# A hybrid decoder layer: the mixers' SBUF in two pools, the SwiGLU's first operands in three groups, and large GpSimd work on VectorE

## The chip, the core and the metric

One core of a Trainium2 chip runs the whole layer. The metric is the device time in microseconds (us) of one execution. The engines are PE (TensorE), DVE (VectorE), ACT (ScalarE), POOL (GpSimd) and SP, which here only issues DMAs; each works through its own queue in order. PEld is the weight load of PE.

## What is computed

```python
h   = x * (1 + scale1) + shift1                 # x: 2048 tokens x 1024
p   = h @ W_in                                  # 26 blocks of 128 columns
mix = concat(conv3_gated(p[:12 blocks]), rwkv7(p[12:])) @ W_out
x   = LayerNorm(alpha * x + (1 + gate1) * mix)
h   = x * (1 + scale2) + shift2
gate, up = split(h @ W_ffn_in)                  # 1024 -> 2 * 2816
x   = LayerNorm(alpha * x + (1 + gate2) * ((silu(gate) * up) @ W_ffn_out))
```

shift, scale and gate come from a small matrix product with c. Everything is float32.

## The kernel before

**Products in three terms.** Each float32 operand is split into a rounded high half and the rest (`split`, L230 to L233: a cast on ACT, then a subtraction), and each product is three matmuls of 128x512. The rest of a weight is `l` for W_in, `lo` for W_out and `wl` for the SwiGLU.

**Mixers.** The tokens come in four quarters of 512. A quarter has projections (`dense`, L256, whose weights `half_weight`, L249, loads and splits) and four units of two RWKV heads each (`unit`, L436), a long chain of small matmuls with DVE and ACT work between them. Within a unit, `kP`, `BK`, `rk` and `R` are products of two 128x512 SBUF tiles. `out_proj` (L301) multiplies a finished quarter by W_out; its matmuls are `do`. Quarters 0 and 1 are projected during the mixers, 2 right behind them, 3 some blocks into the SwiGLU. Normalised and modulated tokens go to DRAM as `h2d`.

**SwiGLU.** Both large products use seven block products instead of eight (`PRODS`, L967). The first product works in two halves of 1024 tokens. `moving` (L1048) loads a half's blocks `b` from `h2d` (four per k, with k from 0 to 3), forms sums and differences of two blocks (`bh`, `us`; L988 on DVE), and splits them into `uh` (ACT) and `ul` (DVE or POOL by turns): 28 operands, two tiles each. Then 22 column blocks run, each seven products of 12 matmuls named `f`; a DVE or ACT instruction takes each product out of PSUM (`c`, L1007).

```python
PRODS = (                                   # product, weight blocks, token blocks
    (3, ("11",), ("12", "-22")),   (5, ("11", "12"), ("22",)),
    (1, ("11", "22"), ("11", "22")), (4, ("22",), ("21", "-11")),
    (7, ("12", "-22"), ("21", "22")), (2, ("21", "22"), ("11",)),
    (6, ("21", "-11"), ("11", "12")))
```

During the second half, `scale_weights` (L1164) loads W_ffn_out in 44 pieces of 128x512 (`wf`, two buffers), multiplies each by the gate's row and stores it to `wfs`.

**What sets the order.** PE's order is written out by `Interleave`, which mixes the projections and the units by a table of assumed delays. For the other engines a scheduler orders the instructions when the program is built. SBUF is given out in pools: `rw` holds all of the mixers' tiles, and after it `fa`, at the same addresses, the SwiGLU's. A tile of `fa` waits for the tiles of `rw` that lay there, and the scheduler gives out the pool after the last of `rw`.

Of the kernel before, what the change touches and what calls it, by code (L numbers as in the profile page):

```python
# [11 lines left out]
F32 = mybir.dt.float32  # L12
F32R = mybir.dt.float32r
AF = mybir.ActivationFunctionType
ALU = mybir.AluOpType
# [4 lines left out]
P = 128  # L20
# [8 lines left out]
QT = S // NQ  # L29
C = 64  # L30
# [41 lines left out]
class Interleave:  # L72
# [31 lines left out]
    def __call__(self, stream, last=True):  # L104

        more = True
        while more or any(last or not t[3] for t in self.tasks):
            if self.side():
                continue
            cost = next(stream, 0) if more else None  # L110
            if cost == 0:
                more = False
            elif cost is not None:
                self.now += cost
            elif self.tasks and not self.side():
                self.now = min(t for t in [t[0] for t in self.tasks] + self.banks if t > self.now)


@with_exitstack
def kernel(  # L120
# [21 lines left out]
    act, dve, pool, pe = nc.scalar, nc.vector, nc.gpsimd, nc.tensor  # L142
# [87 lines left out]
    def split(hi, lo, raw, lo_eng=None):  # L230

        act.copy(out=hi, in_=raw)  # L232
        (lo_eng or pool).tensor_sub(lo, raw, hi)  # L233
# [8 lines left out]
    lnp = ctx.enter_context(tc.tile_pool(name="lnp", bufs=1))  # L242
# [7 lines left out]
    def half_weight(src, name):  # L250

        raw = f512("raw", "r" + name, 3)
        load(out=raw, in_=src)
        wh = f512("wh", "h" + name, 4, F32R)
        wl = f512("wl", "l" + name, 4, F32R)
        split(wh, wl, raw)  # L256
        return wh, wl

    def dense(mov, *tiles):
# [109 lines left out]


    with ExitStack() as ph1:
        rw = ph1.enter_context(tc.tile_pool(name="rw", bufs=1))
        dsc = ph1.enter_context(tc.tile_pool(name="dsc", bufs=1, space=DRAM))


# [16 lines left out]
        uph = rw.tile([P, 512], F32R, name="uph")  # L392
        upl = rw.tile([P, 512], F32R, name="upl")
        gu = rw.tile([P, 512], F32, name="gu")
        blkr = rw.tile([P, P], F32R, name="blkr")

        for tag, bufs in (("yc", 1), ("yo", 1), ("sg", 2)):
            rw.tile([P, QT], F32, tag=tag, name="at" + tag, bufs=bufs)

        carry = rw.tile([P, 2, 14], F32, name="carry")  # L400
        dve.memset(carry, 0.0)
        zcar = rw.tile([P, 4, 2], F32, name="zcar")
# [32 lines left out]
        def c3(ap):  # L435
            return ap.rearrange("p (c t) -> p c t", t=C)  # L436

        def unit(n, q, hp, r, kx, vx, lo):
            u = f"{q}_{hp}"
            th, tl, sg = lo  # L440
# [21 lines left out]
            tz = t2k("tz", "tz" + u)  # L462
# [4 lines left out]
            Pi = t2k("Pi", "Pi" + u)  # L467
            act.activation(Pi, cum, AF.Exp, scale=KAPPA)

            ta = t2k("ta", "ta" + u)  # L470
            act.activation(ta, psa, AF.Tanh, bias=a0h[:, hp:hp + 1], scale=0.5)
            x1, x2 = t2k("nb", "x1" + u), t2k("x2", "x2" + u)
            for x, (m, o) in ((x1, halves[0:2]), (x2, halves[2:4])):
                dve.tensor_scalar(x, ta, m[:, hp:hp + 1], o[:, hp:hp + 1], ALU.mult, ALU.add)
            mk = ta
            act.activation(mk, ta, AF.Identity, scale=kah[:, hp:hp + 1], bias=omka[:, hp:hp + 1])

            sq = t2k("sq", "sq" + u)
# [11 lines left out]
            kP = Pi  # L490
            dve.tensor_tensor(out=kP, in0=Pi, in1=kx, op=ALU.mult)
            BK = rw.tile([P, NC_Q, 2 * C], F32, tag="BK", name="BK" + u, bufs=1)
            dve.tensor_tensor(out=BK[:, :, 0:C], in0=c3(kP), in1=c3(x1), op=ALU.mult)
            pool.tensor_tensor(out=BK[:, :, C:2 * C], in0=c3(kP), in1=c3(x2), op=ALU.mult)

            rk = t2k("sq", "rk" + u)
            pool.tensor_tensor(out=rk, in0=kx, in1=mk, op=ALU.mult)
            dve.scalar_tensor_tensor(out=rk, in0=rk, scalar=vecs[:, V_RK + hp:V_RK + hp + 1], in1=r,
                                     op0=ALU.mult, op1=ALU.mult)
            rkh, rkl = (t2k(tag, f"rk{x}{u}", 1, F32R) for x, tag in (("h", "nb"), ("l", "Pi")))  # L500
# [9 lines left out]
            dve.scalar_tensor_tensor(out=Ak, in0=c3(kx), scalar=nkk[:, hp:hp + 1], in1=Pc[:, :, 0:C],  # L510
                                     op0=ALU.mult, op1=ALU.mult)
            R = rw.tile([P, NC_Q, C], F32, tag="R", name="R" + u, bufs=2)
            pool.tensor_tensor(out=R, in0=c3(r), in1=Pc[:, :, 1:C + 1], op=ALU.mult)


            VU = rw.tile([P, NC_Q, 2, C], F32, tag="VU", name="VU" + u, bufs=2)
# [208 lines left out]
            yo = t2k("yo", "yo" + u)  # L725
# [30 lines left out]
        class Inputs:  # L756


            def __init__(self, q):
                self.q, self.got = q, []  # L760
# [271 lines left out]
        return psum.tile([P, 512], F32, tag=tag, name=name, bufs=bufs)  # L1032

    with ExitStack() as ph2:
        fa = ph2.enter_context(tc.tile_pool(name="fa", bufs=1, reuse_waits="tile"))

        for tag, bufs in (("h26", 8), ("h22", 8), ("h27", 8), ("h24", 8), ("h21", 8), ("h25", 8), ("rawx", 4),
                          ("h23", 8), ("us", 1)):
            fa.tile([P, 512], F32, tag=tag, name="at" + tag, bufs=bufs)
        U = {}  # L1040

        def cycle(*makers):
# [3 lines left out]
        def moving(half):  # L1046

            def operand(i, k, terms, raws, n):  # L1050
                hi, lo = [fa.tile([P, 512], F32R, tag=f"h2{i}", name=f"u{x}{half}_{i}_{k}", bufs=8) for x in "hl"]
                U[half, i, k] = combine(raws, terms, hi, lo, sums, (dve, pool)[n % 2])

            def fetch(t, name, k):
                kk, n = 4 * (int(name[0]) - 1) + k, int(name[1]) - 1
                t0 = half * HT + n * 512
                load(out=t, in_=h2d[kk, :, t0:t0 + 512])
                return t

            def own():  # L1060
                return fa.tile([P, 512], F32, tag="us", name=f"us{half}", bufs=1)

            names = ("12", "22", "11", "21")
            hb = lnp.tile([P, 2, 512], F32, tag="hb", name=f"bh{half}", bufs=1)
            if half == 0:
                sums = cycle(lambda: hb[:, 0, :], lambda: hb[:, 1, :], own)
                for k in range(4):
                    raws = {}
                    for b in names:
                        t = (lnp.tile([P, 512], F32, tag="xr", name=f"b{k}_{b}", bufs=2) if b == "21" else  # L1070
                             fa.tile([P, 512], F32, tag="rawx", name=f"b{k}_{b}", bufs=4))
                        raws[b] = fetch(t, b, k)
                    for n, (i, _, terms) in enumerate(PRODS):
                        operand(i, k, terms, raws, n + k)
                return
            xz = lnp.tile([P, 4, D], F32, tag="xz", name="bz", bufs=1)
            slots = [xz[:, i // 2, i % 2 * 512:(i % 2 + 1) * 512] for i in range(8)] + [hb[:, 0, :], hb[:, 1, :]]
            slots += [lnp.tile([P, 512], F32, tag="xr", name=f"bx{i}", bufs=2) for i in range(2)]
            slots += [temp(f"bt{i}") for i in range(4)]
            sums = cycle(lambda: temp("us"), own)  # L1080
            raws = {k: {} for k in range(4)}
            for b in names:
                for k in range(4):
                    raws[k][b] = fetch(slots.pop(0), b, k)
            yield
            for i, _, terms in PRODS:
                for k in range(4):
                    operand(i, k, terms, raws[k], k)
                yield
# [73 lines left out]
        rw3 = []  # L1163

        def scale_weights():

            for ff in range(FT):
                for m in range(2):
                    ms = slice(m * 512, (m + 1) * 512)
                    w = lnp.tile([P, 512], F32, tag="xr", name=f"wf{ff}_{m}", bufs=2)  # L1170
                    load(out=w, in_=wfo[ff, :, ms])
                    pool.tensor_tensor(out=w, in0=w, in1=rw3[0][:, ms], op=ALU.mult)  # L1172
                    load(out=wfs[ff, :, ms], in_=w)
                    yield

# [239 lines left out]
```

## Time and profile before

| | |
|---|---|
| time, median of 3 runs | 2881.92 us (2880.78 to 2887.45) |
| the profiled execution | 2881.27 us; span of its instructions 2879.5 us |
| PE busy | 2660.8 us, 92% of the span |
| DVE, POOL, ACT busy | 1898.7, 1148.7, 1098.7 us |
| mean granted TensorE clock | 0.955 of 2.4 GHz |
| DMA | 369.86 MB, 128 GB/s over the span |

A time in the text is counted from the first instruction of the span. The mixers run to 1401 us, the SwiGLU's first product from there to about 2390 us, its second to the end. A row that groups instructions gives their line, engine, operation, output<-inputs, shape and count; behind the first bar the busy time in us and the mean ns of one, behind the second the engine's idle time before them and what ended it.

### The profile page before, as it was taken

Reading aid. Unit: us, or ns where it says so; the run is one execution under the profiler, and the core shown is the slowest. Engines: PE = TensorE matmul, PEld = TensorE weight load, DVE = VectorE, ACT = ScalarE, POOL = GpSimd, SP = SyncE. Lnnn points to the kernel's source line nnn. Section 1 sums busy time; section 2 is a strip of 40 time slices with the busy share of each in tenths; the row PEclk is TensorE's granted clock in tenths of the full one; section 3 lists DMA queues with packets and bytes.
Section 4 is the critical chain, followed back from the end, with each engine's and each line's share of the span. In section 5 each row is a group of like instructions: output and inputs, shape, how many; then the busy total and the mean of one; then the engine's idle time right before and its main releaser. Section 6 shows DMA issues by size and latency. Waiting matters only on the chain.

```text
span 2879.5 us, 50206 instructions
## 1 busy us (share of the span) xinstructions
PE 2660.8 (92%) x19232; PEld 2082.8 (72%) x19232; DVE 1898.7 (66%) x3133; ACT 1098.7 (38%) x1995; POOL 1148.7 (40%) x935
## 2 busy tenths in 40 slices
PE   7788999999999899998599999997999999998998
PEld 5566677776777677766477788875767887887786
DVE  7354655556445655554573777788988778659697
ACT  4554433334432433434353533333223333332352
POOL 4665333323333333332453544457886442000011
PEclk8888999989999999999799999998999999999999
DMA  6443322233322222224253533233664336655673
GB/s 236 139 129 116 91 62 70 73 104 119 120 69 69 84 66 69 77 72 156 92 179 128 169 105 106 99 99 121 219 213 138 107 102 222 207 179 186 202 237 106
DMA packets 248344, 369.86 MB, mean 128 GB/s; under 512 B 58660, under 2 KB 81188, under 8 KB 248104
## 3 DMA queue, kind: packets, MB, share of 16 engines
q1 hardware_dynamic: 248104, 366.65, 39.5%
q8 instruction: 151, 2.47, 0.3%
q14 instruction: 89, 0.73, 0.1%
HBM read 278.99 MB, written 87.56 MB: 127 GB/s over the span
## 4 chain that ended last, share of the span: by engine, by line
PE 40%; DVE 5%; DMA 4%; POOL 2%; issue 1%; ACT 0%; SPq 0%; POOLq 0%; DVEq 0%; ACTq 0%
PE f L238 8%; PE f L237 8%; PE f L236 8%; PE o L237 4%; PE o L238 4%; PE o L236 4%; PE do L270 3%; DMA wf<-in_wfo_dram 2%; DMA wfs<-wf 2%; POOL wf L1172 1%; DVE c L1007 1%; DVE ws L988 1%; DMA b<-h2d 0%; DVE ul L233 0%; POOL wl L233 0%
## 5 line engine op out<-in xcount | busy, mean ns | idle before, releaser
L236 PE MATMUL f<-uh,wh 128*128 128x512 f32 x1232 | 495.8, 402 | 32.2 <-ACT uh L232 27.7
L238 PE MATMUL f<-uh,wl 128*128 128x512 f32 x1232 | 495.1, 402 | 19.9 <-POOL wl L233 19.7
L237 PE MATMUL f<-ul,wh 128*128 128x512 f32 x1232 | 494.0, 401 | 12.0 <-DVE ul L233 7.2
L233 POOL TENSOR_TENSOR l<-r,h 128x512 fp32r<-128x512 f32 x201 | 265.2, 1321 | 444.8 <-ACT h L232 359.5
L233 POOL TENSOR_TENSOR wl<-ws,wh 128x512 fp32r<-128x512 f32 x220 | 316.3, 1439 | 296.7 <-ACT wh L232 259.5
L236 PEld LDWEIGHTS f<-uh,wh 128*128 128x128 f32 x1232 | 234.8, 191 | 92.8 <-ACT uh L232 31.8
L238 PEld LDWEIGHTS f<-uh,wl 128*128 128x128 f32 x1232 | 234.8, 191 | 85.6 <-POOL wl L233 30.5
L237 PEld LDWEIGHTS f<-ul,wh 128*128 128x128 f32 x1232 | 234.8, 191 | 72.2 <-DVE ul L233 9.4
L232 ACT CAST wh<-ws 128x512 fp32r<-128x512 f32 x220 | 136.7, 621 | 364.7 <-DVE ws L988 259.0
L1007 DVE TENSOR_TENSOR c<-f,c 128x512 f32<-128x512 f32 x264 | 181.2, 687 | 127.6 <-PE f L238 69.7
L988 DVE TENSOR_TENSOR ws<-w,w 128x512 f32<-128x512 f32 x275 | 242.8, 907 | 18.0 <-DMA w<-wfs 7.4
L237 PE MATMUL o<-ol,fh 128*128 128x512 f32 x616 | 243.3, 395 | 8.9 <-DVE ol L233 8.9
L236 PE MATMUL o<-oh,fh 128*128 128x512 f32 x616 | 242.1, 393 | 4.2 <-DVE c L1007 4.1
L238 PE MATMUL o<-oh,fl 128*128 128x512 f32 x616 | 243.7, 396 | 0.0
L232 ACT CAST h<-r 128x512 fp32r<-128x512 f32 x201 | 123.5, 616 | 215.6 <-PE d L270 157.5
L232 ACT CAST fh<-fr 128x512 fp32r<-128x512 f32 x154 | 95.7, 621 | 237.4 <-PE o L237 160.5
L291 POOL TENSOR_SCALAR rsb<-mvb 128x1 f32<-128x1 f32 x16 | 5.7, 356 | 430.2 <-DVE mvb L289 419.6
L233 DVE TENSOR_TENSOR fl<-fr,fh 128x512 fp32r<-128x512 f32 x154 | 106.2, 693 | 94.1 <-ACT fh L232 85.8
L233 POOL TENSOR_TENSOR lo<-ro,ho 128x512 fp32r<-128x512 f32 x64 | 83.6, 1312 | 198.3 <-ACT ho L232 148.4
L233 POOL TENSOR_TENSOR wl<-w,wh 128x512 fp32r<-128x512 f32 x88 | 127.4, 1448 | 49.4 <-ACT wh L232 49.4
L237 PEld LDWEIGHTS o<-ol,fh 128*128 128x128 f32 x616 | 116.7, 189 | 37.1 <-DVE ol L233 10.6
L236 PEld LDWEIGHTS o<-oh,fh 128*128 128x128 f32 x616 | 116.7, 189 | 31.3 <-DVE c L1007 5.7
(498 smaller groups left out, 5800.1 us busy)
## 6 DMA issues: line engine op xcount, KB each, us to landing
r<-in_win_dram SPq DMA_DIRECT2D x201, 256.0 KB
w<-in_wfi_dram SPq DMA_DIRECT2D x176, 256.0 KB
fr<-fd SPq DMA_DIRECT2D x154, 256.0 KB
w<-wfs SPq DMA_DIRECT2D x132, 256.0 KB
fd<-fs SPq DMA_DIRECT2D x110, 256.0 KB
wm<-in_wmod_dram SPq DMA_DIRECT2D x72, 256.0 KB
ro<-in_wout_dram SPq DMA_DIRECT2D x64, 256.0 KB
fd<-th SPq DMA_DIRECT2D x44, 256.0 KB
```

Of the source, the lines that this page charges most:

```text
L232: act.copy(out=hi, in_=raw)
L233: (lo_eng or pool).tensor_sub(lo, raw, hi)
L236: pe.matmul(ps, lh, rh, start=start, stop=False)
L237: pe.matmul(ps, lh, rl, start=False, stop=False)
L238: pe.matmul(ps, ll, rh, start=False, stop=stop)
L270: pe.matmul(ps, l[:, ks], r, start=kk == 0 and i == 0, stop=kk == KT - 1 and i == 2)
L291: pool.tensor_scalar(rs[:, 0:1], mv[:, 1:2], LN_EPS, None, ALU.add)
L988: (eng or dve).tensor_tensor(out=out, in0=blocks[a], in1=blocks[b.lstrip("-")], op=ALU.subtract if b[0] == "-" else ALU.add)
L1007: dve.tensor_tensor(out=c[b, t], in0=in0, in1=in1, op=op)
L1172: pool.tensor_tensor(out=w, in0=w, in1=rw3[0][:, ms], op=ALU.mult)
```

## The change

There are five edits.

1. The mixers' tiles lie in two pools, `rw` (left) for 20 tags that a unit uses early and `rwb` (right) for the others. `fa` follows at `rw`'s addresses with the loaded blocks `rawx`, one sum tile `us` and the operands of products 3 and 5 (`h23`, `h25`); `fab` follows at `rwb`'s with the other five products' operands. Empty tiles that had fixed the order of addresses are dropped.
2. `moving(0)` makes its operands in three groups, products 3 and 5, then 1 and 4, then 7, 2 and 6, each for all four k, and loads the blocks that a group needs: 8, 12 and 16 loads of 256 KB in place of 16 in all.
3. The low halves of the W_in and W_out weights are made on DVE.
4. In a unit, the second half of `BK`, the first product of `rk` and `R` are made on DVE.
5. The 44 products of `scale_weights` are made on DVE.

```diff
+class Pools:
+    def __init__(self, first, second, early):
+        self.pools, self.early = (second, first), early
+    def tile(self, shape, dtype, name, tag=None, bufs=1):
+        return self.pools[(tag or name) in self.early].tile(shape, dtype, tag=tag or name, name=name, bufs=bufs)
+EARLY1 = ("uph", "upl", "blkr", "Ak", "BK", "x2", "tz", "Pi", "ta", "nb", "sq", "cg", "r", "A", "th", "tl", "k", "v", "z", "AK")
+EARLY2 = ("rawx", "h23", "h25", "us")
...
-        split(wh, wl, raw)
+        split(wh, wl, raw, dve)
...
-        rw = ph1.enter_context(tc.tile_pool(name="rw", bufs=1))
+        rw = Pools(ph1.enter_context(tc.tile_pool(name="rw", bufs=1)),
+                   ph1.enter_context(tc.tile_pool(name="rwb", bufs=1, side="right")), EARLY1)
...
-            pool.tensor_tensor(out=BK[:, :, C:2 * C], in0=c3(kP), in1=c3(x2), op=ALU.mult)
+            dve.tensor_tensor(out=BK[:, :, C:2 * C], in0=c3(kP), in1=c3(x2), op=ALU.mult)
-            pool.tensor_tensor(out=rk, in0=kx, in1=mk, op=ALU.mult)
+            dve.tensor_tensor(out=rk, in0=kx, in1=mk, op=ALU.mult)
...
-            pool.tensor_tensor(out=R, in0=c3(r), in1=Pc[:, :, 1:C + 1], op=ALU.mult)
+            dve.tensor_tensor(out=R, in0=c3(r), in1=Pc[:, :, 1:C + 1], op=ALU.mult)
...
-        fa = ph2.enter_context(tc.tile_pool(name="fa", bufs=1, reuse_waits="tile"))
+        fa = Pools(ph2.enter_context(tc.tile_pool(name="fa", bufs=1, reuse_waits="tile")),
+                   ph2.enter_context(tc.tile_pool(name="fab", bufs=1, reuse_waits="tile", side="right")), EARLY2)
...
-                for k in range(4):
-                    raws = {}
-                    for b in names:
...
-                    for n, (i, _, terms) in enumerate(PRODS):
-                        operand(i, k, terms, raws, n + k)
+                for prods in (PRODS[:2], PRODS[2:4], PRODS[4:]):
+                    for k in range(4):
+                        raws = {}
+                        for b in names:
+                            if any(b in (x.lstrip("-") for x in terms) for _, _, terms in prods):
...
+                        for n, (i, _, terms) in enumerate(prods):
+                            operand(i, k, terms, raws, n + k)
...
-                    pool.tensor_tensor(out=w, in0=w, in1=rw3[0][:, ms], op=ALU.mult)
+                    dve.tensor_tensor(out=w, in0=w, in1=rw3[0][:, ms], op=ALU.mult)
```

PE's order stays as it was but for four small places. On the other queues instructions move; three places follow. In the rows, lines are those of the program shown (the change's are 10 to 14 higher), and a name's last number tells buffers apart.

SP at the end of the mixers, before. `yT<-yg_3` is the store of the last unit's result, `ro` are W_out's weights, `b` the SwiGLU's blocks and `w` its weights:

```order
L1100 DMA w_0_12_15127<-in_wfi_dram 128x512
L1100 DMA w_11_11_15289<-in_wfi_dram 128x512
L734 DMA yT<-yg_3_14536 128x512
L1057 DMA b_12_14955<-h2d 128x512
L1057 DMA b_22_14957<-h2d 128x512
```

And of the change, the stretch from the first blocks on:

```order
L267 DMA ro_5_1_14845<-in_wout_dram 128x512
L1065 DMA b_22_14952<-h2d 128x512
L1065 DMA b_12_14963<-h2d 128x512
...
L267 DMA ro_7_0_14873<-in_wout_dram 128x512
L1065 DMA b_11_15005<-h2d 128x512
...
L745 DMA yT<-yg_3_14536 128x512
L1065 DMA b_11_15055<-h2d 128x512
```

Two blocks (`b_21`) were ahead of that store before; now 18 are, and 18 follow it. The loads of `ro` stand among them.

DVE in the last projection of the mixers, of the change. `lo_4_1` is the low half of W_out that PE's `do` matmuls need next, `S_3` a step of the last unit's state, `mtt` a transposed output of `do`:

```order
L339 SCALAR_TENSOR_TENSOR xz_14673<-xz_14673,mtt_1_14703 128x4x128
L999 TENSOR_TENSOR bh_14949<-b_12_14950,b_22_14952 128x512
L247 TENSOR_TENSOR ul_3_0_14955<-bh_14949,uh_3_0_14954 128x512
L999 TENSOR_TENSOR bh_14949<-b_12_14963,b_22_14965 128x512
L247 TENSOR_TENSOR lo_4_1_14803<-ro_4_1_14800,ho_4_1_14802 128x512
L709 TENSOR_SCALAR S_3_14416<-s_3_14418,Pc_3_13378 128x64
```

Before, this stretch of DVE had only the `S_3` and `xz` rows; `lo_4_1` stood on POOL, and the sums of `b` stood behind the last unit's end.

DVE while W_ffn_out is scaled, of the change. `ws` are sums of weights, `c` takes a product from PSUM:

```order
L999 TENSOR_TENSOR ws_2_7_20409<-w_2_12_20298,w_2_22_20300 128x512
L1182 TENSOR_TENSOR wf_1_21403<-wf_1_21403,rws 128x512
L1018 TENSOR_TENSOR c_2_20426<-f_2_5_20413,c_2_20405 128x512
L999 TENSOR_TENSOR ws_2_2_20434<-w_2_21_20302,w_2_22_20300 128x512
L1182 TENSOR_TENSOR wf_0_21448<-wf_0_21448,rws 128x512
L1018 TENSOR_TENSOR c_2_20405<-f_2_1_20438,c_2_20405 128x512
```

Before, POOL had the `wf` rows, one or two between two `wl`. Now 141 other rows of DVE stand between the first `wf` and the last, 57 of them `c` rows, of which a column block has eight.

## Rows read from the trace of the kernel before

**Rows 1.** The page, part 1: busy us, share of the span, instructions.
```profile
PE 2660.8 (92%) x19232; PEld 2082.8 (72%) x19232; DVE 1898.7 (66%) x3133; ACT 1098.7 (38%) x1995; POOL 1148.7 (40%) x935
```
**Rows 2.** Windows: us, busy per engine (PE, PEld, DVE, ACT, POOL), PEclk, DMA share, GB/s.
```profile
72.00:360.00 288.00, 244.92 (x2384) 187.29 (x2386) 149.15 (x272) 136.91 (x248) 159.32 (x132) 0.88 0.40 119
360.00:1300.00 940.00, 893.85 (x10011) 683.64 (x10007) 516.61 (x1092) 356.75 (x683) 326.56 (x294) 0.97 0.27 81
...
1401.00:1465.00 64.00, 28.81 (x96) 19.86 (x96) 48.72 (x63) 29.76 (x49) 35.74 (x29) 0.65 0.39 130
1465.00:1930.00 465.00, 458.20 (x2006) 369.81 (x2005) 331.20 (x436) 178.94 (x327) 222.01 (x170) 1.00 0.38 126
...
1993.00:2180.00 187.00, 171.73 (x707) 131.98 (x706) 164.75 (x161) 52.69 (x91) 164.38 (x102) 0.99 0.64 215
```
**Rows 3.** Waits of PE, 0 to 1300: who <- whom, us, times, longest.
```profile
PE pz L620 <- DVE LT L613: 14.8, 6, 5.9
PE d L270 <- DVE h_5l L774: 8.0, 2, 5.3
...
PE d L887 <- POOL l L233: 1.9, 2, 1.3
...
PE b L524 <- DVE Ns L597: 0.2, 1, 0.2
```
**Rows 4.** Groups of POOL, 0 to 1296.
```profile
L233 POOL TENSOR_TENSOR l<-r,h 128x512 fp32r<-128x512 f32 x201 | 265.2, 1321 | 444.8 <-ACT h L232 359.5 <-PE d L270 34.1 <-PE s L697 17.6
L233 POOL TENSOR_TENSOR lo<-ro,ho 128x512 fp32r<-128x512 f32 x31 | 41.0, 1327 | 108.9 <-ACT ho L232 97.4 <-PE s L697 8.1 <-PE do L270 3.4
...
L497 POOL TENSOR_TENSOR rk<-k,ta 128x512 f32<-128x512 f32 x16 | 23.6, 1477 | 29.0 <-ACT ta L476 24.7 <-PE ss L484 4.2
```
**Rows 5.** Groups of DVE, 0 to 1296.
```profile
L498 DVE SCALAR_TENSOR_TENSOR rk<-rk,vecs,r 128x512 f32<-128x512 f32 x16 | 23.0, 1438 | 8.9 <-POOL rk L497 8.9
L493 DVE TENSOR_TENSOR BK<-Pi,x 128x512 f32<-128x512 f32 x16 | 21.5, 1342 | 0.1
L572 DVE TENSOR_TENSOR Ym<-sr,kst 128x512 f32<-128x512 f32 x32 | 20.6, 685 | 28.9 <-PE sr L568 28.9
...
L603 DVE TENSOR_TENSOR pr<-G,Ns 128x64 f32<-128x64 f32 x15 | 11.8, 788 | 0.2
```
**Rows 6.** Tile ws, 2450 to 2590, where POOL does nothing: ns min/median/max.
```profile
L988 DVE TENSOR_TENSOR ws<-w,w x17: 683/692/716, 2450.6 to 2586.6; 128x512 f32<-128x512 f32 x17
```
**Rows 7.** Tile ws, 1993 to 2180.
```profile
L988 DVE TENSOR_TENSOR ws<-w,w x42: 677/1760/2755, 1993.1 to 2177.2; 128x512 f32<-128x512 f32 x42
```
**Rows 8.** Timeline of POOL, 1360 to 1400: start, us, instruction, [idle before <-releaser].
```profile
1367.82 1.28 POOL L233 TENSOR_TENSOR lo<-ro,ho 128x512 fp32r<-128x512 f32 x1 [1.85 <-ACT ho L232]
```
**Rows 9.** Timeline of PE, 1398 to 1468.
```profile
1401.06 0.40 PE L270 MATMUL do<-y_7h,lo 128*128 128x512 f32 x1
1408.67 0.80 PE L236 MATMUL f<-uh,wh 128*128 128x512 f32 x1 [7.21 <-ACT uh L232]
...
1446.86 1.09 PE L323 MATMUL mtt<-kst,mt 128*128 128x128 f32 x4 [5.34 <-ACT uh L232]
...
1466.30 0.40 PE L238 MATMUL f<-uh,wl 128*128 128x512 f32 x1
```
**Rows 10.** Timeline of SP's issues, 1380 to 1436.
```profile
1401.75 0.33 SPq L734 DMA_DIRECT2D yT<-yg  x1
1402.12 32.45 SPq L1057 DMA_DIRECT2D b<-h2d  x14
```
**Rows 11.** Tile wf: ns min/median/max, first and last start.
```profile
L1172 POOL TENSOR_TENSOR wf<-wf,rws x44: 1275/1503/1845, 1993.5 to 2179.2; 128x512 f32<-128x512 f32 x44
```
**Rows 12.** The chain that ended last, 2016 to 2100: by line, then pieces (start, us).
```profile
by line: DMA wf<-in_wfo_dram 32.8%; DMA wfs<-wf 32.1%; POOL wf L1172 18.7%; POOL wl L233 5.4%; issue 4.8%; DVE fs L988 4.0%; DVE th L1147 1.3%; SPq L1100 1.0%; SPq L1171 0.8%; SPq L1173 0.4%; SPq L1157 0.4%; POOLq L1172 0.4%; POOLq L233 0.2
...
2044.15 3.41 DMA wfs<-wf
2047.58 3.56 DMA wf<-in_wfo_dram
```

More of the change, by code (lines that the diff above doesn't have):

```diff
@@ L395 @@
         blkr = rw.tile([P, P], F32R, name="blkr")
-        for tag, bufs in (("yc", 1), ("yo", 1), ("sg", 2)):
-            rw.tile([P, QT], F32, tag=tag, name="at" + tag, bufs=bufs)
         carry = rw.tile([P, 2, 14], F32, name="carry")
@@ L1034 @@
     with ExitStack() as ph2:
-        fa = ph2.enter_context(tc.tile_pool(name="fa", bufs=1, reuse_waits="tile"))
-        for tag, bufs in (("h26", 8), ("h22", 8), ("h27", 8), ("h24", 8), ("h21", 8), ("h25", 8), ("rawx", 4),
-                          ("h23", 8), ("us", 1)):
-            fa.tile([P, 512], F32, tag=tag, name="at" + tag, bufs=bufs)
+        fa = Pools(ph2.enter_context(tc.tile_pool(name="fa", bufs=1, reuse_waits="tile")),
+                   ph2.enter_context(tc.tile_pool(name="fab", bufs=1, reuse_waits="tile", side="right")), EARLY2)
         U = {}
@@ L1066, in moving @@
                 sums = cycle(lambda: hb[:, 0, :], lambda: hb[:, 1, :], own)
-                for k in range(4):
-                    raws = {}
-                    for b in names:
-                        t = (lnp.tile([P, 512], F32, tag="xr", name=f"b{k}_{b}", bufs=2) if b == "21" else
-                             fa.tile([P, 512], F32, tag="rawx", name=f"b{k}_{b}", bufs=4))
-                        raws[b] = fetch(t, b, k)
-                    for n, (i, _, terms) in enumerate(PRODS):
-                        operand(i, k, terms, raws, n + k)
+                for prods in (PRODS[:2], PRODS[2:4], PRODS[4:]):
[3 more added lines that the diff above has]
+                            if any(b in (x.lstrip("-") for x in terms) for _, _, terms in prods):
+                                t = (lnp.tile([P, 512], F32, tag="xr", name=f"b{k}_{b}", bufs=2) if b == "21" else
+                                     fa.tile([P, 512], F32, tag="rawx", name=f"b{k}_{b}", bufs=4))
+                                raws[b] = fetch(t, b, k)
+                        for n, (i, _, terms) in enumerate(prods):
+                            operand(i, k, terms, raws, n + k)
                 return
```

## The prediction

> **What bounds the kernel now.** I read the page's first part first: PE is busy 92% of the span and every other engine 66% or less [rows 1]. No matmul goes or comes, so time can only come from PE's idle stretches. The table of windows says where these are [rows 2]: the reader should compare the first number behind the sum (PE) with the window's length. From 72 to 1300 us PE is busy 1138.8 of 1228; from 1401 to 1465 only 28.8 of 64, at a granted clock of 0.65; then 458.2 of 465; from 1993 to 2180 it is 171.7 of 187, while DVE and POOL are each busy some 164. Busy times of matmuls overlap, so I count matmuls instead: 2006 in 465 us are 0.232 us each, a column block of 84 takes 19.5 us, and this is the pace of an undisturbed SwiGLU.
>
> Then the waits of PE in the mixers [rows 3]: the 18 rows that name DVE add to 65 us (the first 14.8, the last 0.2); the low halves made by POOL are waited for 1.9 us in all. PE's timeline after 1401 comes next [rows 9], then SP's [rows 10] and the chain of waits in the scaling stretch [rows 12].
>
> I add up changes to the profiled execution, 2881.27 us, which lies 0.65 under the median of the runs. Some 8.6 us, 0.3%, is what a measurement can tell from no change.
>
> **Transition to the SwiGLU.** Today the last `do` starts at 1401.06, the first `f` at 1408.67, the 84th at 1466.30 [rows 9]: 65 us for 19.5 us of pace, with six idle stretches from 7.21 to 5.34 us, all but the smallest behind the casts of operands. The cause stands on SP [rows 10]: the store of `yT` waits for the last unit until 1401.75, 14 of the 16 loads of `b` stand behind it, and each k's loads wait for the tiles of the k before, so that they are issued over 32.45 us.
>
> The change has eight operands of products 3 and 5 finished before 1401, so PE can begin with two of seven products at once. For the other 20 operands, 18 loads still follow the store; their tiles lie in the second pool, which a late unit holds to the end. Those are 4.7 MB, 22 us at 215 GB/s, the rate of the scaling stretch [rows 2], so to about 1424. DVE is slower: 48.7 us were its work for 28 operands with what stood between them, 20/28 of it is 35 us, so the last operand is ready near 1436. Behind it stand the last two products, 24 matmuls or 5.6 us: 1442. For the last projection I add 5 us: four `lo` that POOL made in 1.28 us as soon as their cast was there [rows 8] now stand on DVE behind sums of blocks whose loads may be late, and PE's `do` wait behind them. So the block ends about 1446: **−20 us**. The lower end is 19.5 us of pace and 3 us of transposes from 1402, 1424: −42. The upper end has 18 loads at today's 2.3 us each (42 us from 1402) and the 31.7 us that lie today between the last issue and the end: 1476, **+10**. The 20 added loads (5.2 MB) are otherwise hidden: they lie beside the last projection, and the mixers move 81 GB/s [rows 2].
>
> **Mixers.** 198 of the 201 low halves of W_in (the three that the start makes stay), 31 of the 64 of W_out [rows 4], and three products in each of 16 units go to DVE, where such an operation takes 0.69 us alone: `Ym`, fed from PSUM, 685 ns [rows 5]; `ws` with two SBUF operands 692 when POOL is idle [rows 6]. So DVE gets 277 x 0.69 = 191 us on top of 666 in 1228 us. It also gets something back. `BK` and `rk` take 1342 and 1438 ns on DVE today, and `pr`, an eighth of their size, 788 [rows 5]; `ws` has a median of 1760 ns when POOL is full [rows 7]. Operations with two SBUF operands stretch while POOL works, and POOL's `l` and `rk`, at 1321 and 1477 ns [rows 4], go away. BK and rk alone would give back 16 x (0.65 + 0.75) = 22 us.
>
> The Trainium skill speaks against this part: its page "Perfetto Trace Analysis", section "Optimizing Scalar/DVE Operations", says that GpSimd and VectorE share an SBUF read port, so that moving work between the two may not help. The stretched `ws` agrees that they get in each other's way; by the rule this term would be 0.
>
> What the sum needs is not DVE's busy time but PE's 65 us of waits for it. Three of a unit's chain operations become 0.7 us shorter, and the halves that now cut into DVE's queue take 0.69 us each where a chain may be waiting. PE's written order hides most of both, so I take a tenth of the waits: **−6 us**. The ends are half of the waits, −33, and all 48 unit products on PE's path at 0.69 us, +33. The `l` themselves cost nothing as long as they come ahead of need, which on POOL they did with 1.9 us of exceptions [rows 3].
>
> **Scaling of W_ffn_out.** The 44 `wf` on POOL start between 1993.5 and 2179.2 [rows 11], two buffers at a time: 8.45 us a pair. The chain says what a pair's cycle is [rows 12]: load 32.8% (2.77 us; single ones up to 3.56), store 32.1% (2.71), POOL's product 18.7% (1.58), waiting behind `wl` 5.4% (0.46), the rest 0.9. On DVE the product takes 0.69 and the `wl` is gone: 8.45 − 0.89 − 0.46 = 7.1; with 0.1 for DVE's own queue, 7.2. DVE's order is fixed, with 141 other rows between the first `wf` and the last; its 57 `c` are 7.1 blocks, 138.5 us of PE at pace. So the stretch takes 22 x 7.2 = 158.4 and PE loses 20 us. Today 707 matmuls, 164 us at pace, take 187: 23 lost. **−3 us**. The lower end has load, store and product alone, 6.2 us a pair: less than PE needs, so nothing lost, −23. For the upper end DVE does its 141 rows at today's contended 1.02 us (164.75/161), 6.6 a pair, two products, 1.4, and stands half a load, 1.4: 9.4 us a pair, or **+45**.
>
> Sum: 2881.27 − 20 − 6 − 3 = **2852 us**.
>
> **The rivals.**
>
> *A, the mixers give back more.* Half of PE's waits for DVE go since POOL leaves the SBUF to it: −20 − 33 − 3, 2825. For it: the stretched BK, rk and pr [rows 5]. Against it: 191 us of new work in the same queue.
>
> *B, the transition's gain is eaten.* The lo of the last projection stand on DVE behind sums that wait for loads, and groups 2 and 3 keep today's rhythm of loads. Then −5 there and nothing in the mixers or the scaling: 2876. For it: every one of those loads stands behind the store of `yT`, as now [rows 10]. In this case the edit does not do what it says: operands are early, the block still ends late.
>
> *C, slower: DVE's queue stands at `wf`.* A product that waits for its load now holds up the `c` that empty PSUM; on POOL only `wl` stood behind it. The price is 22 x (p − 7.2) for a pair's period p. With the other two terms at −26, it costs more than it gave from p = 8.8 and by more than 8.6 us from 9.2; at 9.4 the sum is −26 + 45 = +19, 2900. For it: load and store are two thirds of the chain [rows 12]. Against it: DVE's own work of 5.8 us a pair, uncontended, leaves room.
>
> *D, moving gains nothing in SBUF.* A product on DVE then costs what it cost on POOL, because it holds off POOL's `wl` and is held off by them. The mixers stay, −0, and a pair stays at 8.45: 22 x 8.45 − 138.5 − 23 = +24. With −20 this is +4, 2885. For it: the 1760 ns [rows 7]. Against it: POOL, without the 44 x 1.5 us of `wf`, falls from 164 of 187 us to some 98. This is the rule quoted above.
>
> **How the numbers follow.** The forecast has 0.50; by itself it reaches from 2838 to 2872. A gets 0.17, B 0.11, D 0.09, C 0.13. Faster by over 0.3%: the forecast and A, 0.67. Within 0.3%: B and D, 0.20. Slower: C, 0.13. The range takes in A's time and D's and the nearer part of C's, 2824 to 2890; what is left out is most of C and the far ends of A.
>
> **What would show it.** Transition: the first `f` right behind the last `do`, no wait of PE for `uh` in the first 24 matmuls, the block's 84th near 1446; wrong, if PE waits for `lo` before 1401 or for `uh` as before. Mixers: DVE's `l` near 0.69 us, BK and rk clearly under 1.0, PE's waits for DVE between 33 and 65 us; wrong, if PE waits for `l` by more than some 5 us. Scaling: pairs of `wf` every 7.2 us and `ws` well under 1.7; wrong, if `c` waits show PE held for DVE and the pairs are 9 us apart. The forecast as a whole is wrong if the end of the mixers moves by more than 15 us either way, or if the second product, which the change leaves alone, takes another time than before.

## The result, and the profile after

The change takes 2853.3 us (median of 4 runs, 2848.73 to 2856.61) against 2881.68 of the kernel before: ratio 0.9896, 95% interval 0.9877 to 0.9915. Measured again beside the experiments, the ratio was 0.991 (0.9896 to 0.9924). The forecast was 2852. But the sum came out right while two of its terms did not: the transition gave a fifth of what it should, and a term that was not in the sum at all made up for most of it.

This table cuts the profiled executions at the starts of five matmuls that both kernels have; it is read from PE's timeline of both. "End of W_in" is the last matmul `d` of the projections by W_in; the rest are matmuls `f` and `o`. By it the first product of the kernel before runs to 2427 us, not to about 2390.

| stretch | before, us | after, us | difference | forecast |
|---|---|---|---|---|
| start to the end of W_in | 1222.7 | 1216.1 | −6.6 | −6 |
| to the 84th `f` (end of block 1) | 243.6 | 239.5 | −4.1 | −20 |
| to the end of the first half (block 22) | 479.5 | 473.0 | −6.5 | 0 |
| to the last `f` (second half, with the scaling) | 481.6 | 475.7 | −5.9 | −3 |
| to the last `o` (second product) | 440.2 | 438.6 | −1.6 | 0 |

First part 1 of the page of the change, where [rows 1] were for before: POOL lost 466 us of work, DVE got only 62 more.

```profile
PE 2629.6 (92%) x19232; PEld 2072.2 (73%) x19232; DVE 1961.1 (69%) x3487; ACT 1097.7 (38%) x1995; POOL 682.4 (24%) x581
```

DVE's groups of the change, 0 to 1290, answer to [rows 5]:

```profile
L247 DVE TENSOR_TENSOR l<-r,h 128x512 fp32r<-128x512 f32 x198 | 143.4, 726 | 172.2 <-ACT h L246 153.5 <-PE d L284 10.4 <-ACT Gf L641 7.2
...
L509 DVE SCALAR_TENSOR_TENSOR rk<-rk,vecs,r 128x512 f32<-128x512 f32 x16 | 13.6, 851 | 0.0
...
L505 DVE TENSOR_TENSOR BK<-Pi,x 128x512 f32<-128x512 f32 x16 | 12.0, 752 | 0.0
...
L614 DVE TENSOR_TENSOR pr<-G,Ns 128x64 f32<-128x64 f32 x15 | 5.5, 368 | 0.0
```

The moved `l` take 726 ns each, `BK` fell from 1342 to 752 ns, `rk` from 1438 to 851, `pr` from 788 to 368. So DVE's operations on SBUF did get shorter once POOL had less to do (171 us of work up to the end of W_in in place of 495). The rule that the prediction quoted from the Trainium skill ("Perfetto Trace Analysis", section "Optimizing Scalar/DVE Operations": moving work between the two engines may not help) was not borne out here. It would have given 0 for the mixers where 6.6 us were measured.

Now the transition. PE's timeline of the change, 1364 to 1456, answers to [rows 9]:

```profile
1367.12 1.12 PE L337 MATMUL mtt<-kst,mt 128*128 128x128 f32 x4 [8.31 <-ACT mt L380]
...
1399.53 0.39 PE L284 MATMUL do<-y_7h,lo 128*128 128x512 f32 x1
1399.76 0.39 PE L250 MATMUL f<-uh,wh 128*128 128x512 f32 x1
...
1437.41 0.79 PE L250 MATMUL f<-uh,wh 128*128 128x512 f32 x1 [29.10 <-ACT wh L246]
...
1455.56 0.39 PE L252 MATMUL f<-uh,wl 128*128 128x512 f32 x1
```

The first `f` stands right behind the last `do`, as forecast, and products 3 and 5 run through. Then PE waits 29.1 us, and not for an operand but for `wh`, a weight. SP's timeline of the change says why; [rows 10] were its like before.

```profile
1402.23 0.33 SPq L745 DMA_DIRECT2D yT<-yg  x1
1406.79 11.12 SPq L1065 DMA_DIRECT2D b<-h2d  x10
...
1426.15 5.10 SPq L1065 DMA_DIRECT2D b<-h2d  x3
1432.14 9.41 SPq L1110 DMA_DIRECT2D w<-in_wfi_dram  x6
```

The weight blocks 22 and 21, of which products 1, 4, 7, 2 and 6 need one or both, are loaded from 1432 on, behind all 18 loads of `b`. In the code above, a column block's weight blocks 22 and 21 take the tiles `rawx`, the same four buffers that the blocks `b` pass through.

The 8.31 us at 1367 are the other loss: `mt` stood on ACT behind a cast that waited for a load of `b`, as ACT's timeline of the change shows. The stretch from the end of W_in to the last `do` before block 1 took 183.4 us where it had taken 178.4.

```profile
1364.37 0.62 ACT L246 CAST uh<-b 128x512 fp32r<-128x512 f32 x1 [12.39 <-DMA b<-h2d]
1365.35 0.62 ACT L246 CAST uh<-bh 128x512 fp32r<-128x512 f32 x1 [0.36 <-DVE bh L999]
1365.87 0.61 ACT L246 CAST ho<-ro 128x512 fp32r<-128x512 f32 x1
1366.39 0.68 ACT L380 ACTIVATE mt<-do,pmod 128x512 f32<-128x512 f32 x1
```

Last, the surprise. One row of the windows view of each kernel, 1700 to 1900 us, where PE does nothing but `f` and never waits. The columns are those of [rows 2]; read the number of matmuls in the first bracket. Before:

```profile
1700.00:1900.00 200.00, 200.00 (x859) 161.15 (x858) 152.21 (x200) 66.66 (x114) 94.59 (x73) 1.00 0.29 99
```

The change:

```profile
1700.00:1900.00 200.00, 200.00 (x876) 163.96 (x876) 155.29 (x203) 67.83 (x117) 97.62 (x75) 1.00 0.31 105
```

The same matmuls at the same granted clock of 1.00 follow each other after 228 ns in place of 233. The change's trace tells more: from the start of a product to that of the next, the 12 matmuls of products 3 and 5 take 2800 ns (median), as all seven did before, those of products 4, 7, 2 and 6 take 2720, and product 1 is between (2740). Products 3 and 5 are the ones whose operands lie in the other pool. Over 35 blocks outside the scaling and the first ones that is 0.38 us a block, 13 us.

### The profile page after: what moved, and what is told of

Same layout as the page of the kernel before. It is cut to its first block, busy times and chain, and to the rows that moved or that the text cites. A ratio compares the mean times of both kernels' runs of the same rounds, so it can differ in the third digit from the quotient of the medians.

```text
span 2854.8 us, 50217 instructions
## 1 busy us (share of the span) xinstructions
PE 2629.6 (92%) x19232; PEld 2072.2 (73%) x19232; DVE 1961.1 (69%) x3487; ACT 1097.7 (38%) x1995; POOL 682.4 (24%) x581
## 4 chain that ended last, share of the span: by engine, by line
PE 63%; DVE 9%; DMA 7%; issue 3%; ACT 1%; POOL 1%; SPq 1%; DVEq 0%; POOLq 0%; ACTq 0%
PE d L284 12%; PE f L252 8%; PE f L251 8%; PE f L250 8%; PE do L284 4%; PE o L251 4%; PE o L250 4%; PE o L252 4%; DMA wf<-in_wfo_dram 2%; DMA wfs<-wf 1%; PE w L677 1%; DVE c L1018 1%; DMA yr<-yT 1%; PE s L708 1%; PE sr L579 1%
## 5 line engine op out<-in xcount | busy, mean ns | idle before, releaser
L250 PE MATMUL f<-uh,wh 128*128 128x512 f32 x1232 | 489.5, 397 | 43.3 <-ACT wh L246 41.4
L252 PE MATMUL f<-uh,wl 128*128 128x512 f32 x1232 | 488.5, 397 | 15.0 <-POOL wl L247 14.9
L251 PE MATMUL f<-ul,wh 128*128 128x512 f32 x1232 | 487.3, 396 | 8.2 <-DVE ul L247 4.9
L247 POOL TENSOR_TENSOR wl<-ws,wh 128x512 fp32r<-128x512 f32 x220 | 306.5, 1394 | 385.9 <-ACT wh L246 362.4
L250 PEld LDWEIGHTS f<-uh,wh 128*128 128x128 f32 x1232 | 233.9, 190 | 100.0 <-ACT wh L246 46.4
L247 DVE TENSOR_TENSOR l<-r,h 128x512 fp32r<-128x512 f32 x198 | 143.4, 726 | 172.2 <-ACT h L246 153.5
L999 DVE TENSOR_TENSOR ws<-w,w 128x512 f32<-128x512 f32 x275 | 212.6, 797 | 11.3 <-DMA w<-wfs 5.8
L247 POOL TENSOR_TENSOR wl<-w,wh 128x512 fp32r<-128x512 f32 x88 | 121.6, 1382 | 101.5 <-PE do L284 56.1
L252 PEld LDWEIGHTS o<-oh,fl 128*128 128x128 f32 x616 | 116.8, 190 | 25.3
```

Source lines behind the costliest of these rows:

```text
L250: pe.matmul(ps, lh, rh, start=start, stop=False)
L251: pe.matmul(ps, lh, rl, start=False, stop=False)
L252: pe.matmul(ps, ll, rh, start=False, stop=stop)
L999: (eng or dve).tensor_tensor(out=out, in0=blocks[a], in1=blocks[b.lstrip("-")], op=ALU.subtract if b[0] == "-" else ALU.add)
```

## The experiments

The kernel before took 2876 to 2879 us on the chips of these runs; ratios are to it, with 95% intervals. A stretch is read from one execution: the nine kernels that share the change's moves in the mixers end W_in between 1210.7 and 1217.7 us, so a difference of 2 or 3 us in one stretch alone says little.

**The pace of the matmuls, I.** 64 empty bytes ahead of the SwiGLU's pool, nothing else. In the kernel before, the weights `wh` and `wl` begin at byte 28128 of a partition and the operands at 104352, all tiles being 2048 bytes: their distance, operand minus weights, is 64 modulo 128. In the change it is 64 for products 3 and 5 and 0 for the other five; in this run it is 0 for all. The instructions and their order in the program are those of the kernel before.

```diff
 fa = ph2.enter_context(tc.tile_pool(name="fa", bufs=1, reuse_waits="tile"))
+fa.tile([P, 16], F32, tag="pad", name="pad", bufs=1)
```

> The kernel before with 64 empty bytes ahead of the SwiGLU's pool: every instruction in the same order, only the addresses of the SwiGLU's tiles 64 bytes higher. Theory (the matmuls f became shorter through the address of their moving operand): all seven products take the pace that the change's products 4, 7, 2, 6 show, 2720 ns for 12 matmuls in place of 2801, so 44 blocks x 7 x 81 ns = 25 us less, about 2856, and some 2 us more if the second product gains too. Rival (the pace fell because POOL works less, or differs between chips and not between kernels): 2882, pace 2801.

Measured: 2859.5 us, ratio 0.9939 (0.9925 to 0.9953). The same window of this run:

```profile
1700.00:1900.00 200.00, 200.00 (x884) 165.68 (x883) 148.56 (x209) 66.88 (x114) 97.62 (x73) 1.00 0.32 107
```

12 matmuls take 2720 ns in every product. The pace follows from the address: 64 bytes are worth 17 us. The theory had 25. Some 4.5 us of the 8 missing are the eight blocks beside the scaling, the 24th to the 31st, which took 179.3 us, as before (179.2): the matmuls' pace does not set them.

**The pace, II.** The 64 bytes ahead of the weights' pool instead, so that everything behind moves along.

```diff
 wp = ctx.enter_context(tc.tile_pool(name="wp", bufs=1))
+wp.tile([P, 16], F32, tag="pad", name="pad", bufs=1)
```

> The kernel before with 64 empty bytes ahead of the weights' pool, so that weights and moving operands both lie 64 bytes higher and keep their distance. Theory (the moving operand's own address decides): as in the shift of the SwiGLU's pool alone, about 2856 and 2720 ns for 12 matmuls. Rival (the distance of the weights' address to the moving operand's decides): 2882 and 2801 ns.

Measured: 2878.9 us, ratio 1.0008 (0.9998 to 1.0017), and the window is that of before:

```profile
1700.00:1900.00 200.00, 200.00 (x859) 160.29 (x858) 152.68 (x200) 65.98 (x113) 94.52 (x72) 1.00 0.29 99
```

My theory fell and the rival held: the operands lie where they lay in the run above, yet the pace is the old one. What counts is the distance between a matmul's weights and its moving operand.

**The pace, III.** 32 bytes: a distance of 96.

```diff
+fa.tile([P, 8], F32, tag="pad", name="pad", bufs=1)
```

> The kernel before with 32 empty bytes ahead of the SwiGLU's pool instead of 64: weights and moving operands then differ by 96 modulo 128, after 64 in the kernel before and 0 in the shift by 64. Theory (only a distance of a multiple of 128 is fast): 12 matmuls stay at 2800 ns or above, ratio 0.999 to 1.002. Rival (64 is a bad distance and any other is good): 2720 ns, ratio 0.994.

Measured: 2882.3 us, ratio 1.0016 (1.0004 to 1.0028), again 859 matmuls in the window, 2800 ns for 12. So for `f` 64 and 96 are slow and 0 is fast; other distances were not tried with it. In the second product `o` starts 229 ns after the one before (median) at its old distance of 64, 234 at the 32 of this run, which is where the small loss is, and 227 at 0. So the same distance does not cost the same everywhere.

**The moves alone** (edits 3 to 5, in the kernel before).

> The kernel before with the work moved to VectorE alone (edits 3 to 5), pools and groups as they were. Theory: the mixers give 6 to 7 us, the scaling costs about 3, the transition stays near 65 us, the pace of f stays at 2801 ns for 12: 2877 to 2880, not to be told from before. Rival (lighter POOL shortens the matmuls of the SwiGLU): pace near 2740 and 2860. Rival (the moves are what the whole change lives on): 2855.

Measured: 2868.1 us, ratio 0.9968 (0.9956 to 0.998). W_in ends 5.0 us earlier, the stretch to the end of block 1 is 3.7 shorter, the window has 859 matmuls. So the mixers' gain belongs to the moves and the pace does not. The eight scaling blocks take 181.6 us, 2.4 more. In all it is 8.3 us less on the same chip; the theory had the gain and the scaling's price nearly cancel.

**Pools and groups alone** (edits 1 and 2; the moved work back on POOL).

> The change with the moved work back on POOL: pools and groups alone (edits 1 and 2). Theory: the operands of five products lie at faster addresses, 17 us over the 44 blocks, and the transition gives some 4 to 10: 2855 to 2861; 12 matmuls take 2720 ns in products 4, 7, 2, 6 and 2800 in 3 and 5. Rival (the pace came with the moves): 2801 ns throughout and 2872 to 2878.

Measured: 2868.6 us, ratio 0.9969 (0.9956 to 0.9981). W_in ends at 1223.2, so nothing for the mixers. The window has 875 matmuls, and the halves of the first product are 6.5 us shorter each. The stretch to the end of block 1 takes 243.5 us against 243.6: what the groups were made for brought nothing, and the pace brought 13 us where 17 were expected. The last `do` comes 12 us later than before, and the block after it is 12 us shorter. On the same chip this half of the change is worth 7.8 us and the moves 8.3, together 16, while the whole gives 25 to 28; why the halves do not add up to it was not looked into.

**The weights behind the loads.** The change, with the first column block's weights 22 and 21 in other buffers.

```diff
 raws[b] = (f512("raw", f"w{u}_{b}", 3) if b[0] == "1" else
+           temp(f"w{u}_{b}") if u == f"0_{FFS[0]}" else
            fa.tile([P, 512], F32, tag="rawx", name=f"w{u}_{b}", bufs=4))
```

> The change, with the first column block's weight blocks 22 and 21 loaded into other buffers than those of the token blocks b, so that their loads no longer stand behind all 18 b loads. Theory (PE's 29.1 us before the third product is a wait for these weights): products 1 and 4 run as soon as their operands are there, near 1415 to 1420, the last operand is ready at 1436 as before, the block ends near 1441 to 1445 instead of 1455.6: 11 to 14 us less than the change, ratio to the kernel before 0.985 to 0.986. Rival (the operands end last, as the prediction had it): within 3 us of the change, ratio 0.989 to 0.990, the wait renamed to uh.

Measured: 2850.4 us, ratio 0.9907 (0.9894 to 0.992). The waits of PE, 1395 to 1460, of this run:

```profile
PE f L250 <- ACT uh L246: 9.3, 3, 5.0
PE f L251 <- POOL ul L247: 4.1, 3, 2.9
PE f L251 <- DVE ul L247: 2.5, 2, 1.3
```

The wait of 29.1 us for `wh` is gone, and what is left are the operands, 16 us. Block 1 ends at 1445.7; the stretch from the end of W_in is 231.8 us, 7.7 less than in the change. Yet the ratio is that of the change (0.991): the second half took 479.8 us in place of 475.7, with 182.2 for the scaling blocks.

**The cast that held ACT.** The change, with the eight early operands made on POOL alone.

```diff
+if half == 0 and i in (3, 5):
+    s = raws[terms[0]]
+    if len(terms) > 1:
+        s = sums()
+        plus_minus(s, raws, terms, pool)
+    pool.tensor_copy(out=hi, in_=s)
+    pool.tensor_tensor(out=lo, in0=s, in1=hi, op=ALU.subtract)
+    U[half, i, k] = hi, lo
+    return
 U[half, i, k] = combine(raws, terms, hi, lo, sums, (dve, pool)[n % 2])
```

> The change, with the early operands (products 3 and 5 of the first half: sums, casts, low halves) made on POOL alone. Theory (PE lost 8.3 us in the last projection because ACT's queue stood at a cast that waited for a load of b, with the mt that PE needed behind it): the wait for mt falls to some 1 us, the last unit, its store and all behind it come 7 to 8 us earlier, ratio 0.987. Rival (what held the last projection is PE's work in another order, or DVE): the mt wait only changes its name, ratio 0.989 to 0.990.

Measured: 2859.4 us, ratio 0.9932 (0.9918 to 0.9945). PE's timeline of this run, the waits of 1350 to 1440:

```profile
1359.69 1.09 PE L337 MATMUL mtt<-kst,mt 128*128 128x128 f32 x4 [3.23 <-DVE xz L339]
1435.20 0.80 PE L250 MATMUL f<-uh,wh 128*128 128x512 f32 x1 [35.24 <-ACT wh L246]
```

The wait of 8.31 us behind ACT is gone; 3.23 us behind DVE are left. The last `do` comes 175.4 us after W_in, 8 earlier than in the change. PE then waits 35.2 us instead of 29.1: the store of `yT` was issued at 1401.47 (1402.23 in the change), and the loads follow it. Two of the eight microseconds stay. The scaling blocks took 186.6 us, 7 more than in the change, and the kernel came out no faster than it, rather slower.

**The scaling on POOL again.** The change with one line undone:

```diff
-dve.tensor_tensor(out=w, in0=w, in1=rw3[0][:, ms], op=ALU.mult)
+pool.tensor_tensor(out=w, in0=w, in1=rw3[0][:, ms], op=ALU.mult)
```

> The change, with the 44 products of scale_weights back on POOL. Theory (load and store set the pair's period, and the engine matters little): the eight blocks from the 24th on take 178 to 179.5 us as before and as in the change, the time is that of the change within 3 us. Rival (DVE's queue held at wf costs PE): 4 to 8 us faster than the change. Rival (the product on DVE saves 1.3 us a pair, as the prediction had it): 5 us or more slower.

Measured: 2851.5 us, ratio 0.9911 (0.9899 to 0.9924), 178.6 us for the eight blocks against 179.4 in the change. As the theory had it: in the change's own order the engine hardly matters.

**The three together** (weights, early operands, and 64 bytes ahead of the first pool, so that products 3 and 5 gain the pace too).

> The change with the three things together: first weights 22 and 21 in other buffers, early operands on POOL, and 64 empty bytes ahead of the SwiGLU's first pool so that products 3 and 5 take 2720 ns for 12 matmuls like the others. Theory: the parts add: 12 + 8 + 5 us (2 products x 36 blocks x 76 ns) less than the change, ratio 0.980 to 0.982. Rival (the transition has one bound, so that only the larger of the first two counts): ratio 0.983 to 0.985.

Measured: 2850.4 us, ratio 0.9901 (0.9888 to 0.9914), less than either theory. The pace is 2720 ns in all products and the stretch from W_in to the end of block 1 is 229.0 us, 10.5 less than in the change. All of it was lost in the second half, 486.3 us. The waits of DVE in this run, 1960 to 2165, those of PE, and the row of the windows:

```profile
DVE wf L1193 <- DMA wf<-in_wfo_dram: 26.2, 20, 2.8
```

```profile
PE f L250 <- ACT wh L246: 13.5, 8, 3.1
PE f L252 <- POOL wl L247: 10.1, 10, 3.6
```

```profile
1960.00:2165.00 205.00, 181.43 (x731) 142.75 (x730) 163.06 (x214) 52.90 (x95) 97.41 (x62) 0.94 0.61 203
```

DVE stands 26.2 us at products whose load has not landed. PE waits for no `c`; it waits for `wh` and `wl`, casts and low halves of weights whose sums `ws` stand in DVE's queue among the `wf`. In the change these waits are 7.9 and 9.1 us (1970 to 2160) at a granted clock of 0.99; here they are 6.6 us longer in all, and the clock is 0.94. DVE stands just as long in the change (27.3 us), without this loss. That it depends on the order that the scheduler gave DVE is argued, not shown.

**The same, with the scaling on POOL.**

> The change with first weights 22 and 21 in other buffers, early operands on POOL, 64 empty bytes ahead of the SwiGLU's first pool, and the products of scale_weights back on POOL. Theory (what these three gained in the transition and in the pace was lost again in the scaling stretch, because DVE's queue stands at a wf that waits for its load): the eight blocks from the 24th on take 177 to 180 us instead of 191.8, all else as in the run of the three together, so about 12 us less than it, 2838, ratio 0.985 to 0.987. Rival (the stretch is paced by loads and stores whoever multiplies): 188 us and more, ratio 0.990.

Measured: 2845.1 us, ratio 0.9881 (0.9864 to 0.9897). The eight blocks take 179.6 us instead of 191.8, the second half 476.0 instead of 486.3, as expected, and PE's wait for `wh` in this stretch is gone. The median fell by 5 us, not 12, and the intervals of the two ratios overlap; the gain is clear in the stretch, not in the time. In this profile the stretch from W_in to the end of block 1 is 232.6 us, 3.6 longer.

**And the early operands back on ACT and DVE.**

> As the last, but with the early operands on ACT and DVE as in the change. Theory (the early operands on POOL give 8 us before the SwiGLU and keep only what the loads behind the store of yT don't take back, some 2 us): 0 to 4 us slower than the last kernel, block 1 ends 2 us later against the end of the projections. Rival (the two parts of the transition add): 8 us slower.

Measured: 2842.65 us, ratio 0.9876 (0.986 to 0.9893): the lowest median, not to be told from the last run, against 2853.4 for the change on the same chip. W_in to the end of block 1 is 232.0 us, so early operands on POOL give nothing that shows.

**The change once more.**

> The change itself once more, beside the kernels it is compared with. By every theory the ratio to the kernel before is that of the first measurement, 0.988 to 0.992; it is run because the kernel before has taken 2876 to 2882 us on the chips so far and the parts to be told apart are of some 5 to 10 us.

Measured: 2853.4 us, ratio 0.991 (0.9896 to 0.9924); every stretch of the table is within 2 us of the first profile.

## Why the prediction was right, and where it was not

**The total.** 2852 was forecast and 2853.3 measured. The profile's −24.7 is −6.6 for the mixers, −4.1 for the transition, and −14.0 for the three stretches behind, where the forecast had −3 and where the scaling's own part is near 0. An error of 16 us and one of 11 the other way cancelled; that the medians come within 2 us of the forecast is luck.

**The transition, −20, was −4.** The step that failed is "the last operand is ready near 1436. Behind it stand the last two products". The operands were ready: the last cast `uh` started at 1435.19. (That time came by another road than the forecast's: from 1402 to 1436 DVE is busy for 23.6 us, not 35, while the last load of `b` is issued at 1430.93 and not by 1424.) What I had not counted are the weights that those products multiply. I followed the 18 loads of `b` through SP and their buffers, but not who else takes these buffers: the weight blocks 22 and 21 wait for the last `b` to be used, and stand behind it on SP.

How much of the 16 missing us this is shows when the end of block 1 is counted from the store of `yT`, behind which the loads stand. Before, it ends 64.5 us after the store; the prediction had 44 (1402 to 1446); in the change it is 53.3, and in the run with other buffers for the weights 46.4. So the weights cost 7 us, and without them the prediction of this part holds within 3. Another 7 are the store itself. It is issued 179.0 us after the end of W_in before and 186.1 after it in the change; 185 to 191 in every run with the pools and groups, 175 to 180 in every run without. The sum took the mixers' gain and the transition as terms that add; but the store came at 1402.23, no earlier than before (1401.75), so the loads saw nothing of the 6.6 us. What makes the store late is not shown; it is as late (185.9) in the run without the wait of 8.31 us. That block 1 ends at 1445.7 in the run with other buffers, where the prediction had 1446, is chance: W_in ended 8.8 us earlier there than in the kernel before.

So rival B's sentence, operands early and the block still late, came true through a mechanism that it did not name. The 5 us for the last projection are what the balance shows (183.4 against 178.4), but they were put on the wrong engine: the order showed `lo` on DVE behind sums, but the 8.3 us came on ACT, by the same cause, a row in the queue that waits for a load. The moves alone shorten that projection, to 173.6; the pools and groups cost it 10 us.

**The pace was taken as fixed.** The step "this is the pace of an undisturbed SwiGLU" is 0.232 us in [rows 2], and I let it stand for every block of the change. The change gives tiles other addresses, and five of seven products became 2 to 3% faster. The trace of the kernel before held no more than a hint: its `do`, matmuls of the same shape at a distance of 0, follow each other after 227 ns (median of those without a wait) and its `f` after 233; but its `d`, at a distance of 0 too, after 231. What could have been asked is why 200 us without a wait hold 859 matmuls, and with which addresses.

**The mixers, −6, were −6.6, but not for the reason given.** I took a tenth of PE's waits for DVE. These waits did not fall: rows that name DVE add to 60 us up to the end of W_in, 59 before. What fell is PE's busy time in that stretch, by 10 us. The windows of the kernel before, of the change, and of the change once more:

```profile
0.00:1222.70 1222.70, 1121.67 (x11825) 859.71 (x11826) 674.87 (x1402) 495.52 (x937) 495.33 (x440) 0.94 0.32 99
```

```profile
0.00:1216.10 1216.10, 1111.81 (x11825) 852.50 (x11826) 750.48 (x1664) 496.50 (x937) 171.22 (x178) 0.95 0.33 100
```

```profile
0.00:1214.90 1214.90, 1113.26 (x11825) 853.92 (x11826) 751.28 (x1664) 496.89 (x937) 170.31 (x178) 0.94 0.34 100
```

In all runs it is 1115 to 1122 us with the mixers' work on POOL and 1110 to 1118 with it on DVE, so part of these 10 us is chance. The granted clock differs little, and in the third row not at all, so it is not what gives the gain. In single places it changes with the waits. PE's timeline of the kernel before, then its windows:

```profile
841.83 1.65 PE L620 MATMUL pz<-LT,Np 64*64 64x64 f32 x26 [5.88 <-DVE LT L613]
```

```profile
836.00:840.00 4.00, 0.00 (x0) 0.00 (x0) 0.92 (x3) 1.86 (x5) 1.26 (x1) 1.00 0.18 22
840.00:845.00 5.00, 3.17 (x64) 3.13 (x64) 1.77 (x3) 1.13 (x3) 1.27 (x1) 0.58 0.52 174
845.00:850.00 5.00, 5.00 (x47) 3.81 (x44) 0.45 (x1) 1.74 (x6) 0.00 (x0) 0.74 0.03 10
```

And PE's timeline and a window of the change at the same work:

```profile
834.97 0.97 PE L631 MATMUL pz<-LT,Np 64*64 64x64 f32 x26 [0.18 <-DVE LT L624]
```

```profile
840.00:845.00 5.00, 5.00 (x51) 3.92 (x52) 2.02 (x4) 3.43 (x10) 0.00 (x0) 1.00 0.31 93
```

The wait of 5.88 us went, and with it the stretch in which the clock was at its lower level for part of the time, a mean of 0.58 and then 0.74. Elsewhere a wait came: 5.70 us for `LT` at 427.97, none before. Which of PE's work became shorter is not shown. All five kernels with the mixers' work on POOL end W_in at 1222.7 to 1223.9, and all nine with it on DVE at 1210.7 to 1217.7, so the sign is sure; that I got the size from a tenth of the waits is luck.

**The scaling, −3, was near 0.** In the change the eight blocks take 0.2 us more than before and 0.8 more than with `wf` on POOL. The pair's period was to be 7.2 us, 1.25 shorter. Tile `wf` of the change:

```profile
L1182 DVE TENSOR_TENSOR wf<-wf,rws x44: 677/693/2403, 1975.6 to 2142.9; 128x512 f32<-128x512 f32 x44
```

That is 7.78 us a pair from first start to last, 167.3 us for 43 steps, and the product itself 693 ns as taken. The prediction had divided the 185.7 us of the kernel before by 22 pairs in place of 21.5; counted alike they are 8.64, not 8.45, so a pair became 0.86 us shorter. Rival C was nearer than its 0.13 looked: in the change DVE's stand at `wf` costs nothing, but three runs in which only the transition or the pace was altered lost 3 to 12 us in these blocks, and in the two runs with `wf` back on POOL the loss was gone. For the largest of the three that is a test of the cause; for the other two it is argued. By PE's waits the way from `wf` to PE was another than C's, over the sums `ws` and not the `c`. C's bounds were also worked out wrong: by its own formula the change costs more than it gave from a pair of 8.5 us, not 8.8, and by more than 8.6 us from 8.9, not 9.2. Rival A did not come, nor D: `ws` has a median of 684 ns in this stretch, 1760 before [rows 7].

**What stays open.** Why a distance of 64 or 96 bytes costs an `f` some 6 ns was not looked into, nor which order of DVE's rows decides whether a late `wf` reaches PE, nor what delays the store of `yT` with the pools and groups.

## What to carry to other kernels

When a transfer is moved ahead, list everything that shares its buffers and its queue, not only the data itself: here the next product's weights stood behind loads that had been counted, and operations that wait for an early load held up an in-order queue that PE needed. If a change gives tiles other addresses, compare the number of matmuls in a stretch without waits before and after. An operation that waits for a load is best put on an engine that nothing urgent follows.

## What the runs showed that I had not expected

A matmul `f` of 128x512 follows the one before after 227 ns where weights and moving operand lie a multiple of 128 bytes apart, and after 233 ns at distances of 64 and 96 bytes modulo 128; for `o` it is 227, and 229 at 64. Moving one pool by 64 bytes made the kernel before 0.6% faster with every instruction in its old order. And a wait of PE can cost more than its length: behind the 5.88 us at 836 the next ten microseconds ran at granted clocks of 0.58 and 0.74, where the change, without the wait, ran at 1.00.
